# A hybrid attention and mixture-of-experts block: a block's rows dealt over sixteen runs, and the late experts' weight loads put in another order

## The chip, the cores and the metric

One core of one Trainium2 chip runs the whole block. The metric is the device time of one execution in microseconds (us). Before the change it is 1148.38 us, the median of 3 runs (1148.19 to 1149.16). One further execution was profiled; every duration below comes from it.

## The reference, cut to what matters

The block first mixes tokens (a gated linear attention branch and an indexer-selected attention branch, joined by gates and an output projection), and then adds a mixture of experts. Only the second part is touched:

```python
def hier_moe(h, w_rg, b_rg, w_re, b_re, w_gate, w_up, w_down):   # h: 1024 tokens of 1024
    ...
    g_sel = jnp.argmax(g_logits, axis=-1)                        # one of 4 groups
    ...
    top_v, top_i = lax.top_k(e_in_group, EXPERT_TOPK)            # two of its 8 experts
    ...
    for e in range(N_EXPERTS):                                   # 32
        hid = jax.nn.silu(xf @ w_gate[e]) * (xf @ w_up[e])       # w_gate, w_up: 1024 x 128
        y = y + combine[:, e:e + 1] * (hid @ w_down[e]).astype(f32)   # w_down: 128 x 1024
    return y.astype(h.dtype).reshape(b, t, d)
```

Each token picks 2 experts, so 32 experts share 2,048 rows, 64 on average. Worked out from the reference on its own inputs, an expert gets between 44 and 93 rows; the last one to be computed gets 63, the one before it 90, the first one 48. All in fp32.

## The kernel before

**The block of an expert.** A block is a table of R = 96 row numbers for each of the 32 experts, one number to a partition. `place` fills it: a token that is the r-th of its expert is compared with the constant row `self.slot` (part of `onehot`, made in `_constants`, L85), and a product on TensorE puts the token's number into that partition whose `slot` equals r. Before the change `slot` is 0, 1, 2, ... 95, so an expert with 64 tokens fills partitions 0 to 63, and partitions 64 to 95 hold an out-of-range number. An expert with over 96 tokens would leave its rest to a loop at the end of `run`, which works from another table and is not entered with these inputs.

**Work of one expert** (`Moe.run`, the loop over j = 0 to 31, in the order `self.order`). An indirect DMA issued from GpSimd (`gather_x`, L1275) fetches the tokens' rows of 4 KB from `h2d` into 96 partitions; a row with an out-of-range number is not moved. TensorE transposes them (`xpose`, L1283). `split` (L1259 on ScalarE, L1260 on VectorE) turns the raw gate and up weights into a high and a low part in two buffers. `gate_up` (L1267) is 24 matmuls of 256 columns; then come the activation, a transpose (`hid_T`, L1303) and `down` (L1311), 4 matmul instructions on the raw down weights. A second indirect DMA (`scatter`, L1319) adds the rows, 4 KB each, to `out` in memory, again leaving out those out of range. The order of one step j is: `gate_up(j+1)`, `hid_T(j)`, `xpose(j+2)`, `gather_x(j+5)`, `down(j)`, `scatter(j)`, `split(j+2)`, `load(j+9)`.

**The weights.** An expert has three loads of 512 KB (`load`): gate (L1023), up (L1026), down (L1029), all issued on SP's queue. There are NR = 9 buffers, so the load of expert j+9 needs the buffer of expert j: its gate and up halves are free once `split(j)` has read them, its down part only after `down(j)`. Gate and up also wait until a gather issued shortly before has landed (`late`). SP issues strictly in its order, and the tile framework gives its DMAs eight semaphores in turn, so an issue also waits until the load eight places ahead in SP's order has landed in full. The order on SP is made by the framework's scheduler from the program's order and from what each load waits for; a `SCHED` dependency between two instructions only fixes which stands first.

```python
        first = q = nc.sync.dma_start(raw[0][:, 0:1024], wg...)         # gate
        q = nc.sync.dma_start(raw[0][:, 1024:2048], wu...)              # up
        self.down = nc.sync.dma_start(raw[1], wd)                       # down
```

Of the kernel before, what the change touches and what calls it, by code (L numbers as in the profile page):

```python
# [21 lines left out]
SCHED = mybir.DependencyInfo(mybir.DependencyClass.NoSync, mybir.DependencyReason.SCHED_ONLY)  # L22
# [5 lines left out]
NT = T // P  # L28
# [5 lines left out]
R = 96  # L34
OOB = 1 << 20
NE = 32
# [7 lines left out]
def _bucket(rel):  # L44
    n = np.abs(rel)
    nf = np.maximum(n, 1).astype(np.float32)
    large = 8 + (np.log(nf / np.float32(8)) / np.float32(math.log(16.0)) * np.float32(8)).astype(np.int32)
    large = np.minimum(large, 15)
    return np.where(rel > 0, 16, 0) + np.where(n < 8, n, large)
# [12 lines left out]
def _constants():  # L62
    c = np.zeros((P, C_W), np.float32)
    p = np.arange(P)

    def put(name, v):
        o, w = _OFF[name]
        c[:, o:o + w] = v

    put("ident", np.eye(P))  # L70
    same = (p[:, None] // 64) == (p[None, :] // 64)
    put("suf", (p[:, None] > p[None, :]) & same)
    put("lt", p[:, None] < p[None, :])
    put("ones", 1.0)
    put("cmask", np.where((p[:, None] < 64) & (p[None, :] >= 64), NEG, 0.0))
    put("ind2", (p[:, None] // 64) == np.arange(2)[None, :])
    put("iota_e", np.arange(NE)[None, :])
    put("tok", p[:, None] + P * np.arange(NT)[None, :])
    put("tie8", 8 - np.arange(8)[None, :])
    put("tie4", 4 - np.arange(4)[None, :])  # L80
    put("thr", (np.arange(NB) + 1)[None, :] * R)
    put("pid", p[:, None])
    oh = np.zeros((P, 512 + R + NT), np.float32)
    oh[:, 384:512] = np.eye(P)[::-1]
    oh[:, -R - NT:-NT] = np.arange(R)[None, :]  # L85
    oh[:, -NT:] = p[:, None] + P * np.arange(NT)[None, :] - T
    rel = np.arange(383) - 255
    oh[_bucket(rel), np.arange(383)] = 1.0
    oh[15, :384] -= 1.0
    oh[15, 383] = 0.0  # L90
    return c, oh
# [893 lines left out]
class Moe:  # L985
# [27 lines left out]
        assert self.ko <= 20.75 * 256  # L1013
        return a

    def load(self, j, wg=None, wu=None, wd=None, late=None, after=None):
        nc = self.nc
        if wg is None:
            e = self.order[j]
            wg, wu, wd = self.w_gate[e], self.w_up[e], self.w_down[e]  # L1020
        raw = self.raws[j % len(self.raws)]

        first = q = nc.sync.dma_start(raw[0][:, 0:1024], wg.rearrange("(p k) c -> p (k c)", p=P))  # L1023
        if late:
            self.tc.add_manual_dep(q.ins, late.ins.name, SYNC, reason="the tokens' rows come first")
        q = nc.sync.dma_start(raw[0][:, 1024:2048], wu.rearrange("(p k) c -> p (k c)", p=P))  # L1026
        if late:
            self.tc.add_manual_dep(q.ins, late.ins.name, SYNC, reason="the tokens' rows come first")
        self.down = nc.sync.dma_start(raw[1], wd)  # L1029
        for q in (first, q, self.down) if after else ():  # L1030
            self.tc.add_manual_dep(q.ins, after.ins.name, SCHED, reason="order of loads")
        return raw
# [213 lines left out]
    def run(self, vp, ch, dump, stop):  # L1246
# [8 lines left out]
        def split(j, raw, late=False):  # L1255
            hi, lo = (t.rearrange("p (k n c) -> p n k c", k=KT, n=2) for t in WG[j % 2])
            for n in range(2):
                r = raw[0][:, 1024 * n:1024 * n + 1024].rearrange("p (k c) -> p k c", k=KT)
                nc.scalar.activation(hi[:, n], r, AF.Copy)  # L1259
                q = nc.vector.tensor_sub(lo[:, n], r, hi[:, n].bitcast(F32))  # L1260
                if late:
                    tc.add_manual_dep(q.ins, self.routed.ins.name, SCHED, reason="routing first")
# [9 lines left out]
        gathered = {}  # L1272

        def gather_x(j, idx):
            gathered[j] = nc.gpsimd.indirect_dma_start(out=XG[j % 4][:R], out_offset=None, in_=self.h2d,  # L1275
                                         in_offset=bass.IndirectOffsetOnAxis(ap=idx, axis=0),
                                         bounds_check=T - 1, oob_is_err=False)
            return gathered[j]

        def xpose(j):  # L1280
            pt = self.bankA(f"pxg{j}").rearrange("p a (b t) -> p (a b) t", b=4)
            xg = XG[j % 4]
            qs = [nc.tensor.transpose(pt[:, k, :R], xg[:R, k * P:(k + 1) * P], ident[:R, :R]) for k in range(KT)]  # L1283
            xh, xl = (t.rearrange("p (k t) -> p k t", k=KT) for t in XT[j % 2])
            nc.scalar.activation(xh, pt[:, :, :R], AF.Copy)  # L1285
            self.xl = nc.vector.tensor_sub(xl, pt[:, :, :R], xh.bitcast(F32))  # L1286
            return qs[0]

        def gate_up(j):
            w = [t.rearrange("p (k c) -> p k c", k=KT) for t in WG[j % 2]]  # L1290
            x = [t.rearrange("p (k t) -> p k t", k=KT) for t in XT[j % 2]]
            pg = self.bankB(f"pgu{j}")
            last = mm3(pg[:R, :256], [([t[:, k, :] for t in x], [t[:, k, :] for t in w]) for k in range(KT)])
            th, hd = HD[j % 2][:, 0:P], HD[j % 2][:, P:2 * P]
            nc.scalar.activation(th[:R], pg[:R, :P], AF.Tanh, scale=0.5)  # L1295
            nc.vector.scalar_tensor_tensor(hd[:R], th[:R], 1.0, pg[:R, :P], op0=ALU.add, op1=ALU.mult)
            nc.vector.tensor_mul(hd[:R], hd[:R], pg[:R, P:256])
            return last

        def hid_T(j):  # L1300
            hd, hT = HD[j % 2][:, P:2 * P], HD[j % 2][:, 2 * P:3 * P]
            ph = self.bankC(f"phd{j}")
            nc.tensor.transpose(ph[:, :R], hd[:R], ident[:R, :R])  # L1303
            nc.scalar.activation(hT[:, :R], ph[:, :R], AF.Copy)  # L1304

        def down(j, raw, wgt):
            hT = HD[j % 2][:, 2 * P:3 * P]
            for half in range(2):
                py = self.bankB(f"py{j}{half}")
                s = slice(512 * half, 512 * half + 512)  # L1310
                nc.tensor.matmul(py[:R], hT[:, :R], raw[1][:, s], start=True, stop=True)  # L1311
                av = AC[j % 4][:R, s]
                if half:
                    nc.scalar.activation(av, py[:R], AF.Copy, scale=wgt)  # L1314
                else:
                    nc.vector.tensor_scalar(av, py[:R], wgt, None, op0=ALU.mult)  # L1316

        def scatter(j, idx):
            return nc.gpsimd.indirect_dma_start(out=self.out, out_offset=bass.IndirectOffsetOnAxis(ap=idx, axis=0),  # L1319
                                                in_=AC[j % 4][:R], in_offset=None, bounds_check=T - 1, oob_is_err=False,  # L1320
                                                compute_op=ALU.add)

        def apart(a, g):

            for q in range(4):
                if q != g:
                    for b in done.get(q, []):
                        tc.declare_no_dep(a.ins, b.ins, reason="tokens of another group")
            done.setdefault(g, []).append(a)
# [8 lines left out]
        NR = len(self.raws)  # L1338
# [10 lines left out]
        first = gate_up(0)  # L1349
# [3 lines left out]
        for j in range(NE):  # L1353
            if j + 1 < NE:
                gate_up(j + 1)
            hid_T(j)
            if j + 2 < NE:
                xpose(j + 2)
                if j + 5 < NE:
                    gather_x(j + 5, idx(j + 5))  # L1360
            down(j, raw(j), wgt(j))
            apart(scatter(j, idx(j)), self.order[j] // 8)
            if j + 2 < NE:
                split(j + 2, raw(j + 2))
            if j + NR < NE:
                self.load(j + NR, late=gathered.get(min(j + 3, NE - 1)) if j > 1 else None)
            if j == 4:
                self.blocks(dump)
            if j == 9:
                tc.add_manual_dep(nc.gpsimd.drain().ins, gathered[j + 5].ins.name, SCHED, reason="after the gather")  # L1370
            if j == NE - 3:
                ntot = nc.values_load(self.lrow[0:1, 3:4], min_val=0, max_val=24)  # L1372
# [48 lines left out]
```

## Time and profile before

| what | us or share |
|---|---|
| median of 3 runs | 1148.38 (1148.19 to 1149.16) |
| the profiled execution, its own time | 1146.56 |
| its span, first to last instruction | 1144.8 |
| TensorE (PE) busy | 1077.3, 94% |
| VectorE (DVE) busy | 880.6, 77% |
| ScalarE (ACT) busy | 502.7, 44% |
| GpSimd (POOL) busy | 299.4, 26% |
| mean granted TensorE clock | 0.977 of full speed |
| time on the DMA engines of SP's loads and stores (q1) | 29.5% of 16 engines |
| the same of GpSimd's DMAs (q0) | 6.7% of 16 engines |

The shares are averages over a long program; the experts are its last fifth, from about 930 us on. A share of DMA is the time that packets took, over 16 DMA engines. The profile gives no engine's own share, only their mean, and a load has landed only when the slowest of its 16 engines is done.

### The profile page before, as it was taken

Reading aid. Unit: us, or ns where it says so; the run is one execution under the profiler, and the core shown is the slowest. Engines: PE = TensorE matmul, PEld = TensorE weight load, DVE = VectorE, ACT = ScalarE, POOL = GpSimd, SP = SyncE. Lnnn points to the kernel's source line nnn. Section 1 sums busy time; section 2 is a strip of 40 time slices with the busy share of each in tenths; the row PEclk is TensorE's granted clock in tenths of the full one; section 3 lists DMA queues with packets and bytes.
Section 4 is the critical chain, followed back from the end, with each engine's and each line's share of the span. In section 5 each row is a group of like instructions: output and inputs, shape, how many; then the busy total and the mean of one; then the engine's idle time right before and its main releaser. Section 6 shows DMA issues by size and latency. Waiting matters only on the chain. (4 is left out here: it accounts for less than half of the span.)

```text
span 1144.8 us, 18016 instructions
## 1 busy us (share of the span) xinstructions
PE 1077.3 (94%) x6652; PEld 895.1 (78%) x6652; DVE 880.6 (77%) x1742; ACT 502.7 (44%) x1110; POOL 299.4 (26%) x240
## 2 busy tenths in 40 slices
PE   6999999899999999999989999999999859999785
PEld 5998898788788888989767878887777747777563
DVE  5679999999999999994487786373566758878563
ACT  6566627032221124653588775121222226666352
POOL 0110025231122120312043210052011255487332
PEclk9999999999999999999999999999999959999898
DMA  7111120134223221200001015486442578999894
GB/s 260 38 38 38 38 75 4 48 103 164 74 91 111 92 79 51 74 1 1 19 20 38 19 39 186 147 282 211 147 147 83 186 251 228 300 314 265 251 289 81
DMA packets 73133, 139.81 MB, mean 122 GB/s; under 512 B 12315, under 2 KB 47444, under 8 KB 73044
## 3 DMA queue, kind: packets, MB, share of 16 engines
q1 hardware_dynamic: 62772, 112.40, 29.5%
q0 software_dynamic: 7968, 17.86, 6.7%
q10 hardware_dynamic: 2304, 8.39, 1.9%
q8 instruction: 53, 0.87, 0.3%
q14 instruction: 36, 0.29, 0.1%
HBM read 115.24 MB, written 31.76 MB: 128 GB/s over the span
## 5 line engine op out<-in xcount | busy, mean ns | idle before, releaser
L747 DVE MAX8 G<-G 128x8 f32<-128x384 f32 (+5 forms) x192 | 171.1, 893 | 5.0
L748 DVE MATCH_REPLACE8 G<-G 128x384 f32<-128x384 f32 (+5 forms) x192 | 168.1, 876 | 0.0
L236 PE MATMUL pg<-Qa,Q 128*128 128x512 f32 x512 | 159.8, 392 | 0.0
L228 POOL TENSOR_TENSOR Q<-G,Q 128x2048 fp32r<-128x2048 f32 x13 | 60.1, 4626 | 210.5 <-ACT Q L227 210.5
L236 PEld LDWEIGHTS pg<-Qa,Q 128*128 128x128 f32 x512 | 96.0, 188 | 20.9 <-issue 0.9
L236 PE MATMUL pg<-Qb,Q 128*128 128x512 f32 x256 | 99.6, 389 | 0.0
L227 ACT ACTIVATE Q<-G 128x2048 fp32r<-128x2048 f32 x19 | 36.3, 1911 | 78.4 <-PE pg L236 76.8
L236 PE MATMUL pv<-Q,Qa 128*128 128x256 f32 x352 | 65.0, 285 | 0.0
L1319 POOL DMA_INDIRECT out_dram<-G x24 | 47.7, 1986 | 64.8 <-ACT G L1314 21.2
L630 POOL TENSOR_TENSOR sm<-Tb,G 128x256 f32<-128x256 f32 x48 | 35.3, 738 | 98.4 <-DVE G L648 64.3
L1267 PE MATMUL pgu<-Qb,xt1h 128*96 128x256 f32 x256 | 52.9, 305 | 4.3 <-ACT xt1h L1285 3.7
L236 PEld LDWEIGHTS pv<-Q,Qa 128*128 128x128 f32 x352 | 55.2, 191 | 1.5 <-issue 1.0
L1260 DVE TENSOR_TENSOR Qb<-G,Qb 128x1024 fp32r<-128x1024 f32 x38 | 45.7, 1216 | 13.7 <-ACT Qb L1259 13.2
L236 PEld LDWEIGHTS pg<-Qb,Q 128*128 128x128 f32 x256 | 48.1, 188 | 10.4 <-issue 0.5
L1267 PE MATMUL pgu<-Qb,xt0h 128*96 128x256 f32 x256 | 53.7, 311 | 0.9 <-issue 0.9
L1275 POOL DMA_INDIRECT xg<-h2d,G x32 | 47.0, 1467 | 26.4 <-PE pxg L1283 8.1
L653 ACT ACTIVATE sm<-sm,G 128x128 f32<-128x128 f32 (+7 forms) x64 | 49.3, 772 | 7.0 <-DVE G L648 6.5
L1267 PEld LDWEIGHTS pgu<-Qb,xt1h 128*96 128x96 f32 x256 | 39.2, 175 | 14.6 <-ACT xt1h L1285 13.6
L236 PE MATMUL pv<-Q,Qb 128*128 128x256 f32 x176 | 49.7, 283 | 0.0
L814 POOL TENSOR_TENSOR G<-G 128x512 f32<-128x512 f32 x16 | 24.3, 1526 | 92.4 <-DVE G L813 92.4
L662 PE MATMUL pPT<-G,sm 128*128 128x128 f32 x288 | 44.6, 279 | 2.7 <-ACT sm L653 1.1
L577 ACT ACTIVATE G<-pg 128x1024 f32<-128x1024 f32 x16 | 16.3, 1019 | 69.2 <-issue 41.4
(369 smaller groups left out, 2982.5 us busy)
## 6 DMA issues: line engine op xcount, KB each, us to landing
G<-in_w_in_dram SPq DMA_DIRECT2D x19, 1024.0 KB
G<-in_w_down_dram SPq DMA_DIRECT2D x19, 512.0 KB
G<-in_w_gate_dram SPq DMA_DIRECT2D x19, 512.0 KB
G<-in_w_up_dram SPq DMA_DIRECT2D x19, 512.0 KB
gd<-G SPq DMA_DIRECT2D x16, 512.0 KB
G<-gd SPq DMA_DIRECT2D x16, 512.0 KB
raw<-in_w_gate_dram SPq DMA_DIRECT2D x9, 512.0 KB
raw<-in_w_up_dram SPq DMA_DIRECT2D x9, 512.0 KB
```

The source lines that it names most:

```text
L227: nc.scalar.activation(hi, r3, AF.Copy)
L228: (eng or nc.vector).tensor_sub(lo, r3, f(hi))
L236: q = nc.tensor.matmul(o, a, b, start=(i == 0), stop=(i == len(seq) - 1))
L630: nc.gpsimd.tensor_tensor(band, Tb[:, h, :], sc[i][:, n1:], op=ALU.add)
L653: nc.scalar.activation(sm[:, :W], sm[:, :W], AF.Exp, scale=-1.0, bias=nm[:, 1:2], accum_out=rs8s[i][:, h:h + 1])
L662: nc.tensor.transpose(pt[:, b, :], sm[:, (b0 + b) * P:(b0 + b + 1) * P], ident)
L747: nc.vector.max(out=m8, in_=sc[i])
L748: nc.vector.match_replace(out=sc[i], in_to_replace=m8, in_values=sc[i], imm_value=SENT)
L1260: q = nc.vector.tensor_sub(lo[:, n], r, hi[:, n].bitcast(F32))
L1267: q = nc.tensor.matmul(o, a, b, start=(i == 0), stop=(i == len(seq) - 1))
L1275: gathered[j] = nc.gpsimd.indirect_dma_start(out=XG[j % 4][:R], out_offset=None, in_=self.h2d, in_offset=bass.IndirectOffsetOnAxis(ap=idx, ...
L1319: return nc.gpsimd.indirect_dma_start(out=self.out, out_offset=bass.IndirectOffsetOnAxis(ap=idx, axis=0), in_=AC[j % 4][:R], in_offset=Non ...
```

## The change

Two edits. First, `slot` becomes a deal: partition s takes the token of rank (s mod 6) * 16 + s div 6. The 96 partitions are seen as sixteen runs of six, and ranks 0 to 15 go to the first partition of each run, 16 to 31 to the second, and so on. An expert with 64 tokens now has four rows in each run of six, at partitions 0 to 3, 6 to 9, 12 to 15 and so on. Second, from expert 18 on (counted from 0) each gate load is made to stand behind the down load of the expert ahead, and each down load behind the up load of its own expert.

```diff
     oh[:, 384:512] = np.eye(P)[::-1]
-    oh[:, -R - NT:-NT] = np.arange(R)[None, :]
+
+    s = np.arange(R)
+    oh[:, -R - NT:-NT] = (s % (R // 16) * 16 + s // (R // 16))[None, :]
     oh[:, -NT:] = p[:, None] + P * np.arange(NT)[None, :] - T
...
-    def load(self, j, wg=None, wu=None, wd=None, late=None, after=None):
+    def load(self, j, wg=None, wu=None, wd=None, late=None, after=None, turns=False):
...
+        if turns:
+
+            self.tc.add_manual_dep(first.ins, self.down.ins.name, SCHED, reason="the expert ahead comes first")
         self.down = nc.sync.dma_start(raw[1], wd)
+        if turns:
+            self.tc.add_manual_dep(self.down.ins, q.ins.name, SCHED, reason="the expert's parts in order")
...
-                self.load(j + NR, late=gathered.get(min(j + 3, NE - 1)) if j > 1 else None)
+                self.load(j + NR, late=gathered.get(min(j + 3, NE - 1)) if j > 1 else None, turns=j + NR >= 18)
```

On PE, VectorE, ScalarE and GpSimd the two programs have the same instructions in the same order. On SP the loads are the same, in another order from expert 18 on. The first place is SP's queue in the middle of the loop. `in_w_gate`, `in_w_up` and `in_w_down` are the sources; `rawx`, `raw5`, `raw6` and `raw7` are the buffers of the experts that leave a remainder of 2, 5, 6 and 7 by 9, and `G` holds the other five. Before, from the gate load of expert 18 on:

```order
L1023 DMA G_69<-in_w_gate_dram 128x1024
L1026 DMA G_69<-in_w_up_dram 128x1024
L1029 DMA raw7_7767<-in_w_down_dram 128x1024
L1023 DMA G_69<-in_w_gate_dram 128x1024
L1026 DMA G_69<-in_w_up_dram 128x1024
L1029 DMA G_69<-in_w_down_dram 128x1024
L1023 DMA rawx_6642<-in_w_gate_dram 128x1024
L1026 DMA rawx_6642<-in_w_up_dram 128x1024
L1029 DMA G_69<-in_w_down_dram 128x1024
```

These are gate and up of expert 18, down of 16 (`raw7`), gate and up of 19, down of 17, gate and up of 20 (`rawx`), down of 18, and so on: gate and up go two experts ahead of down. After the change, the same place, beginning with down of 15 (`raw6`):

```order
L1034 DMA raw6_7554<-in_w_down_dram 128x1024
L1028 DMA G_69<-in_w_up_dram 128x1024
L1034 DMA raw7_7767<-in_w_down_dram 128x1024
L1028 DMA G_69<-in_w_up_dram 128x1024
L1034 DMA G_69<-in_w_down_dram 128x1024
L1025 DMA G_69<-in_w_gate_dram 128x1024
L1028 DMA rawx_6642<-in_w_up_dram 128x1024
L1034 DMA G_69<-in_w_down_dram 128x1024
L1025 DMA G_69<-in_w_gate_dram 128x1024
L1028 DMA G_69<-in_w_up_dram 128x1024
L1034 DMA G_69<-in_w_down_dram 128x1024
L1025 DMA rawx_6642<-in_w_gate_dram 128x1024
```

The order is now up 18, down 16, up 19, down 17, gate 18, up 20, down 18, gate 19, up 21, down 19, gate 20 (`rawx`). Up and down stand where they stood; a gate load has moved two experts back, to the place that the gate of the expert after next had. The second place is the end of SP's queue. Before, from gate and up of expert 30 on:

```order
L1023 DMA G_69<-in_w_gate_dram 128x1024
L1026 DMA G_69<-in_w_up_dram 128x1024
L1029 DMA G_69<-in_w_down_dram 128x1024
L1023 DMA G_69<-in_w_gate_dram 128x1024
L1026 DMA G_69<-in_w_up_dram 128x1024
L1029 DMA rawx_6642<-in_w_down_dram 128x1024
L1029 DMA G_69<-in_w_down_dram 128x1024 x2
```

After, from the gate load of expert 29 (`rawx`) on:

```order
L1025 DMA rawx_6642<-in_w_gate_dram 128x1024
L1028 DMA G_69<-in_w_up_dram 128x1024
L1034 DMA rawx_6642<-in_w_down_dram 128x1024
L1025 DMA G_69<-in_w_gate_dram 128x1024
L1034 DMA G_69<-in_w_down_dram 128x1024
L1025 DMA G_69<-in_w_gate_dram 128x1024
L1034 DMA G_69<-in_w_down_dram 128x1024
```

Before, up of 31 was the last load ahead of three downs. Now the gates of 30 and 31 stand between these downs, and gate 31 is the last load but one.

## Rows read from the trace of the kernel before

**Rows 1.** The page's 40 slices of the span: TensorE, clock, DMA engines
```profile
PE   6999999899999999999989999999999859999785
PEclk9999999999999999999999999999999959999898
DMA  7111120134223221200001015486442578999894
```

**Rows 2.** Stretches: length, busy time by engine (count), clock, DMA share, GB/s
```profile
960.00:1055.00 95.00, 93.86 (x647) 73.71 (x646) 76.79 (x105) 62.69 (x106) 61.78 (x35) 1.00 0.95 285
1055.00:1075.00 20.00, 17.85 (x123) 13.95 (x122) 12.66 (x18) 9.36 (x15) 9.25 (x6) 1.00 0.88 253
1075.00:1095.00 20.00, 14.72 (x76) 10.73 (x75) 9.99 (x14) 8.72 (x14) 5.44 (x4) 0.74 0.89 261
1095.00:1115.00 20.00, 16.61 (x100) 12.25 (x97) 12.53 (x18) 11.17 (x20) 6.54 (x4) 0.91 0.93 303
```

**Rows 3.** Timeline of PE: where gate and up of experts 5, 21, 31 begin
```profile
965.17 0.56 PE L1267 MATMUL pgu<-Qb,xt1h 128*96 128x256 f32 x2
...
1052.87 0.56 PE L1267 MATMUL pgu<-Qb,xt1h 128*96 128x256 f32 x2
...
1124.30 0.80 PE L1267 MATMUL pgu<-Qb,xt1h 128*96 128x256 f32 x2
```

**Rows 4.** Waits of ScalarE from 1055 to 1115: total, times, longest
```profile
ACT Qb L1259 <- DMA G<-in_w_gate_dram: 7.9, 3, 3.8
ACT Qb L1259 <- DMA raw<-in_w_gate_dram: 4.9, 2, 3.8
ACT Qb L1259 <- DMA raw<-in_w_up_dram: 4.6, 2, 2.7
ACT Qb L1259 <- DMA G<-in_w_up_dram: 3.0, 2, 2.1
```

**Rows 5.** Waits of SP's queue from 1040 to 1110, its first three
```profile
SPq L1023 <- DMA raw<-in_w_up_dram: 9.6, 3, 3.4
SPq L1023 <- DMA G<-in_w_up_dram: 8.9, 4, 3.4
SPq L1029 <- DMA raw<-in_w_gate_dram: 8.8, 3, 3.0
```

**Rows 6.** Timeline of SP: gates of experts 14, 25, 26, 27, 30; up of 31
```profile
973.02 0.34 SPq L1023 DMA_DIRECT2D raw<-in_w_gate_dram  x1
...
1046.39 0.33 SPq L1023 DMA_DIRECT2D raw<-in_w_gate_dram  x1
...
1056.67 0.33 SPq L1023 DMA_DIRECT2D G<-in_w_gate_dram  x1
...
1066.91 0.33 SPq L1023 DMA_DIRECT2D G<-in_w_gate_dram  x1
...
1093.75 0.33 SPq L1023 DMA_DIRECT2D G<-in_w_gate_dram  x1
...
1102.33 0.33 SPq L1026 DMA_DIRECT2D G<-in_w_up_dram  x1
```

**Rows 7.** DMA queues from 973 to 1118: packets, MB, share of 16 engines
```profile
q1 hardware_dynamic: 7873, 28.67, 57.2%
q0 software_dynamic: 5104, 12.08, 35.3%
```

**Rows 8.** The same from 1003 to 1010, when only weights flow
```profile
q1 hardware_dynamic: 738, 2.69, 96.9%
```

**Rows 9.** A stretch in which the last scatter alone runs, columns as above
```profile
1137.20:1138.20 1.00, 0.00 (x0) 0.00 (x0) 0.00 (x0) 0.00 (x0) 0.00 (x0) 0.50 0.60 115
```

**Rows 10.** The longest wait of PE from 915 to 965
```profile
PE pxg L1283 <- DMA xg<-h2d,G: 5.4, 1, 5.4
```

**Rows 11.** Timeline of ScalarE: the split of expert 31's weights
```profile
1118.07 1.99 ACT L1259 ACTIVATE Qb<-G 128x1024 fp32r<-128x1024 f32 x2
```

**Rows 12.** Chain that ended last: split of expert 30, matmuls of expert 29
```profile
1111.80 1.07 ACT Qb L1259
...
1114.03 0.96 DVE xt1l L1286
...
1115.03 2.83 PE pgu L1267 x22
```

## Prediction
> **What bounds the kernel now.** I read the page's slices first, then stretches of the experts' part, then who waits for whom, then the DMA queues.
>
> The slices [rows 1] show TensorE near full until the last six or seven, where it falls to 5 to 8 tenths, the clock dips, and the DMA engines are at their busiest. The stretches [rows 2] sharpen this: from 960 to 1055 TensorE is busy 93.86 of 95 us; in the three stretches of 20 us behind it 17.85, 14.72 and 16.61, and the granted clock falls to 0.74 and 0.91, that is, part of the time at 1.2 instead of 2.4 GHz, behind TensorE's idle time. So two stages: first TensorE is the bound, then something else.
>
> What it loses is read from three starts [rows 3]. Experts 5 to 21 begin from 965.17 to 1052.87, 16 steps of 5.48 us. Ten more steps from 1052.87 would let expert 31 begin at 1107.7; it begins at 1124.30. The late stage costs **16.6 us**, the clock's part included. What TensorE lacks are weights: ScalarE's split waits 7.9 + 4.9 + 4.6 + 3.0 = 20.4 us for gate and up loads between 1055 and 1115 [rows 4].
>
> Why are loads late? SP issues a load only when one issued earlier has landed [rows 5], and does so every 3.42 us (six loads between 1046.39 and 1066.91 [rows 6]). But an engine has 8 packets of 4 KB in a load. When only weights flow, 2.69 MB, 657 packets, take 96.9% of 16 engines for 7 us [rows 8]: 0.165 us a packet, 1.3 us a load. At the same time the engines' mean share is 0.88 to 0.95 [rows 2], at 253 to 303 GB/s. Loads that wait while engines have time left mean that a few engines are late and each load waits for them.
>
> The gathers and scatters can do this. If the 96 partitions are served in order, six to an engine, ranks 0 to 41, which every expert has (44 at least), fill the first seven engines, while the last five get little. A full engine then has 6 rows where the mean is 4. Check: from 973 to 1118 the queues moved 28.67 MB of weights and 12.08 MB of rows [rows 7], per engine 437 packets and 184 rows. A row took 35.3% x 145 x 16 / 2949 = 0.278 us. A full engine: 437 x 0.165 + 276 x 0.278 = 72 + 77 = 149 us, against the 145 that passed. I take this as the bound: seven or eight engines, full throughout. With the weight packets' price in this mixture, 57.2% x 145 x 16 / 7000 = 0.190 us, it would be 160, 10% too long; 0.165 is nearer.
>
> **The change, part by part.**
>
> *The deal.* It moves no byte, instruction or wait; each expert's rows spread over the sixteen runs, at most one row apart. By the experts' counts the fullest engine falls from 192 of the 2,048 rows to 143, the mean is 128. Fullest engine from 973 on: 72 + 184 x 143/128 x 0.278 = 72 + 57 = 129 us, scaled by what the check missed (145/149), **126 us: the last weights land at about 1099** instead of 1118. Bounds: evenly spread, 120 us, 1093; with 0.190 a packet, 83 + 57 = 140 us, 1113.
>
> *When they are needed.* At TensorE's pace expert 31 begins at 1107.7. Its split began 6.2 us ahead of its matmuls (1118.07 [rows 11], 1124.30 [rows 3]), so its gate is wanted at **1101.5**. I allow nothing beyond that: the chain [rows 12] runs from the split of expert 30 over VectorE's `xt1l` to the matmuls of expert 29, because ScalarE and VectorE work in order, and a late gate holds up the expert ahead of it too.
>
> *The order of loads.* What SP's queue holds is not quite what the words say: gate j stands behind down j-1, but up j and down j have stayed, so a gate comes two experts, six loads, later than before, and up waits for it idle. No wait is added: the down that a gate now follows is due to its buffer long before. But in a queue that is behind, six loads are time: 126 us over 56 loads is 2.25 us each, 13.5 us in the middle. There gate 28 has nine loads behind it, lands near 1099 - 20 = 1079, and is needed at 1101.5 - 3 x 5.48 = 1085; gate 25, with eighteen behind it, at 1059 for 1069. At the end gate 31 has one load behind it, where up 31 had three: it lands at about 1097, 4 us ahead of need, where the old order would have had 9. With the bound of 1113 it lands at 1111, 10 us late; with 1093, in time. I take **2 us** of new stalls, nearer the second, since the check favours 0.165.
>
> *The ends.* The first gather holds TensorE for 5.4 us [rows 10]; expert 0's 48 rows put 3 on an engine instead of 6, among other packets. At 0.165 to 0.278 a row that is 0.5 to 0.8 us, up to twice that if weight packets alternate with them, nothing if they are not the last: 0 to 1.5, I take 0.5. The last scatter has 63 rows, 4 instead of 6 in the fullest run. With it alone, 115 GB/s are 28 rows in a microsecond on 0.60 of 16 engines [rows 9], 0.34 us a row: 0.7 us saved at the very end (0.5 to 1). That share fits 63 rows dealt six to an engine (10.5 of 16, 0.66) better than an even spread.
>
> *The sum:* 1146.56 (the profiled execution) - 16.6 - 0.7 - 0.5 + 2 = **1130.8**. That execution is 1.8 us under the median, within what single runs differ by; I put the forecast at **1131.5**.
>
> *A rule against it.* The row: the mean share of 0.60 with one scatter of 63 rows running [rows 9], and the 145 us that six rows to an engine nearly explain [rows 7]. The Trainium skill's page "DMA: Bandwidth & Descriptors", section "The descriptor swizzle", says that in a transfer of 128 partitions engines 0 to 7 serve partitions 0 to 63, in groups of four, and 8 to 15 the rest. If that held for these 96, runs of six would be no engine's share, and the deal would spread the rows only in part; by it the sum would be that of the third rival.
>
> **The rivals.**
>
> 1. *Weights stay the bound.* With 0.190 us a packet, gate 31 lands at 1111, 10 us after 1101.5: 1146.56 - 16.6 - 1.2 + 10 = 1139, with the median's offset **1140**. For it: the DMA share is at 0.93 from 1095 to 1115 already, little room if all that time is real work. Against: the check fits the lower price.
>
> 2. *Slower: the deal relieves nothing, and late gates cost.* If the full engines stay full, gate 25, issued at 1046.39, goes where gate 27 went, 1066.91 [rows 6], 20 us later, and at the end the gate of 30, once issued at 1093.75, stands behind up 31, issued at 1102.33. That one was there for its split by 1119 or so [rows 11], 7 us after the split of expert 30 began [rows 12]. A microsecond may hide: 1148.4 + 6 = **1154**. It decides if the fullest engine gains less than about 4 us in 145. For it: no view shows single engines. Against: the share under 1 while every load is waited for, and the check.
>
> 3. *Rows dealt by groups of four.* Partitions 0 to 63 on eight engines: before, 8 of 64 rows on each of these, 72 + 368 x 0.278 = 174 us, 20% over what passed, so the rows speak against it. After, four of every six partitions are filled, 5.3 rows an engine: 72 + 245 x 0.278 = 140 us, the last weights at 1113 and **1140**. This is what the skill's swizzle would make of this kernel.
>
> 4. *The two edits cancel:* relief of 4 to 8 us, spent by later gates: **1148**.
>
> **How the numbers follow.** About 0.2%, 2.3 us, is what a measurement of this kernel can tell from no change. The forecast, 1126 to 1135, gets 0.67; rival 1 0.16, rival 3 0.04, rival 2 0.08, rival 4 0.05. Faster: 0.67 + 0.16 + 0.04 = 0.87; same 0.05; slower 0.08. The low end is the sum without new stalls, with the larger gains at both ends (16.6 + 1.0 + 1.5, so 1127.5) and the median no higher than a profiled execution, rounded down to 1126; the high end takes in rivals 1 and 3 and stops short of rivals 2 and 4: 1142.
>
> **What would show it.** Right: expert 31 begins near 1107 to 1109; from 1055 to 1110 TensorE is as busy as before 1055 and the clock stays at 1.00; ScalarE's waits for gate and up loads fall from 20.4 us to a few; SP issues a load every 2.2 to 2.5 us and GB/s rise over 300; the last weights land at 1095 to 1105. The waits that remain should name gates, not ups, since gates are what the new order makes late. Wrong: SP still spaced by 3.4 us (the deal relieves nothing, rival 2), or a high DMA share with splits waiting for gates (rival 1), or a new wait of TensorE on gathers.

## The result, and the profile after

The changed kernel takes 1131.97 us (median of 4 runs, 1130.81 to 1134.32) against 1148.29 us for the kernel before in the same comparison (4 runs, 1146.62 to 1149.16): a ratio of 0.9862, 95% interval 0.9842 to 0.9883. Its profiled execution took 1132.71 us. The forecast of 1131.5 is 0.5 us off, and that is partly luck: two of its terms were wrong in opposite directions, as the experiments show.

The slices of the page after, against [rows 1]: in slice 38 TensorE rises from 7 to 9 tenths, the clock from 8 to 9 and the DMA engines from 8 to 9. The dip of slice 33 is in both; a slice is some 28 us long, so that one lies ahead of expert 5.

```profile
span 1130.9 us, 18002 instructions
...
PE   6999999899999999999999999999999959999985
...
PEclk9999999999999999999999999999999979999998
DMA  8111120125222321200000112565543297999993
```

The stretches, with the columns of [rows 2]: length, busy time by engine with counts, clock, DMA share, GB/s.

```profile
960.00:1055.00 95.00, 93.88 (x642) 73.28 (x640) 77.01 (x106) 62.81 (x107) 62.75 (x36) 1.00 1.03 311
1055.00:1075.00 20.00, 17.72 (x123) 13.57 (x121) 14.07 (x19) 12.20 (x20) 10.18 (x7) 1.00 1.05 322
1075.00:1095.00 20.00, 19.00 (x133) 15.27 (x133) 14.52 (x21) 11.42 (x21) 8.55 (x5) 1.00 1.03 330
1095.00:1115.00 20.00, 17.79 (x105) 13.54 (x103) 11.67 (x17) 9.06 (x17) 7.09 (x4) 0.91 0.40 89
```

The DMA engines move 311 to 330 GB/s in the first three stretches, where it was 253 to 285, and the bytes are through earlier: from 1095 on the DMA share is 0.40. TensorE is nearly full again from 1075 to 1095, but not from 1055 to 1075 nor behind 1095. Where expert 5 and expert 31 begin their matmuls, against the first and last of [rows 3]:

```profile
962.01 0.56 PE L1274 MATMUL pgu<-Qb,xt1h 128*96 128x256 f32 x2
...
1111.26 0.80 PE L1274 MATMUL pgu<-Qb,xt1h 128*96 128x256 f32 x2
```

That is 149.25 us for these 26 steps, after 159.13 before: 9.9 us of the span's 13.9 us. Another 3.2 us were saved ahead of expert 5, and 0.9 us behind the start of expert 31 (19.6 us to the end of the span, after 20.5). Expert 31 began at 1111.26, later than the 1107 to 1109 that the prediction gave as a sign. What ScalarE still waits for, from 1055 to 1115, against [rows 4] (engine and line, what it waited for, total, times, longest):

```profile
ACT Qb L1266 <- DMA G<-in_w_gate_dram: 5.4, 4, 2.3
ACT Qb L1266 <- SPq L1383: 2.1, 1, 2.1
ACT Qb L1266 <- DMA raw<-in_w_gate_dram: 0.4, 1, 0.4
```

20.4 us of waits for gate and up loads have become 5.8 us for gates, and none names an up load. The 2.1 us that the view puts down to SP's branch stand ahead of the split of expert 29 and are a gate's too: that gate was issued at 1073.46 and landed 18.7 us later, at 1092.2, as the split began. So the waits for gates come to 7.9 us.

```profile
1073.46 0.33 SPq L1025 DMA_DIRECT2D rawx<-in_w_gate_dram  x1
...
DMA to landing us min/median/max: 18.7/18.7/18.7
```

The timeline of ScalarE:

```profile
1083.82 1.06 ACT L1266 ACTIVATE Qb<-G 128x1024 fp32r<-128x1024 f32 x1 [0.83 <-DMA G<-in_w_gate_dram]
...
1092.28 2.01 ACT L1266 ACTIVATE Qb<-rawx 128x1024 fp32r<-128x1024 f32 x2 [2.10 <-SPq L1383]
1097.22 1.06 ACT L1266 ACTIVATE Qb<-G 128x1024 fp32r<-128x1024 f32 x1 [2.06 <-DMA G<-in_w_gate_dram]
...
1105.03 1.99 ACT L1266 ACTIVATE Qb<-G 128x1024 fp32r<-128x1024 f32 x2
```

These are the splits of experts 28, 29, 30 and 31. Those of 28 to 30 begin after an idle time; that of 31 does not.

### The profile page after: what moved, and what is told of

It reads as the page before. It is cut to its first block, busy times and chain, and to the rows that moved or that the text cites. A ratio compares the mean times of both kernels' runs of the same rounds, so it can differ in the third digit from the quotient of the medians.

```text
span 1130.9 us, 18002 instructions
## 1 busy us (share of the span) xinstructions
PE 1071.0 (95%) x6652; PEld 891.3 (79%) x6652; DVE 879.9 (78%) x1742; ACT 502.0 (44%) x1110; POOL 301.2 (27%) x240
## 4 chain that ended last, share of the span: by engine, by line
PE 66%; DVE 16%; DMA 10%; issue 4%; ACT 4%; SPq 0%; POOL 0%; POOLq 0%; DVEq 0%; ACTq 0%
PE pg L238 15%; PE py L238 8%; PE pw L238 5%; PE pgu L1274 5%; DVE G L750 4%; DVE G L749 3%; PE pav L677 3%; PE pqkv L238 3%; DMA G<-in_w_up_dram 3%; PE pPT L664 3%; PE pidx L238 3%; PE pv_None L238 2%; DMA raw<-in_w_gate_dram 2%; DVE G L419 2%; PE pk L238 2%
## 5 line engine op out<-in xcount | busy, mean ns | idle before, releaser
L1282 POOL DMA_INDIRECT xg<-h2d,G x32 | 50.9, 1590 | 24.9 <-DVE xt1l L1293 12.7
L1274 PE MATMUL pgu<-Qb,xt1h 128*96 128x256 f32 x256 | 50.4, 294 | 5.1 <-ACT xt1h L1292 5.1
```

What stands on the lines that cost most here:

```text
L1274: q = nc.tensor.matmul(o, a, b, start=(i == 0), stop=(i == len(seq) - 1))
```

## The experiments

Each table entry "5 to 31" is the time from the first matmul of expert 5 to that of expert 31 in the profiled execution, read from two rows like those above. It leaves out the start of the expert stage, which differs by up to 2.3 us between two executions of one kernel (below).

| kernel | rows | order of loads | median us | ratio to before, 95% interval | 5 to 31, us |
|---|---|---|---|---|---|
| before | in order | old | 1148.29 | 1 | 159.1 |
| the change | dealt | new | 1131.97 | 0.9862 (0.9842 to 0.9883) | 149.3 |
| the change, again | dealt | new | 1133.37 | 0.9892 (0.9876 to 0.9909) | 147.7 |
| deal only | dealt | old | 1126.15 | 0.9830 (0.9814 to 0.9845) | 141.9 |
| deal only, again | dealt | old | 1126.84 | 0.9824 (0.9807 to 0.9840) | 141.9 |
| order only | in order | new | 1151.29 | 1.0047 (1.0032 to 1.0063) | 165.0 |
| mirrored | in order, from the far end | old | 1141.37 | 0.9957 (0.9940 to 0.9974) | 155.6 |
| rotated | in order, from run 4 on | old | 1143.67 | 0.9971 (0.9952 to 0.9989) | 157.2 |
| dealt over 12 runs | dealt in part | old | 1139.88 | 0.9935 (0.9910 to 0.9960) | 151.5 |
| strict order | dealt | gate, up, down | 1131.28 | 0.9852 (0.9821 to 0.9882) | 144.7 |
| back and forth | dealt evenly | new | 1130.49 | 0.9854 (0.9830 to 0.9879) | 145.4 |
| back and forth, no wait for gathers | dealt evenly | old | 1125.29 | 0.9825 (0.9800 to 0.9851) | 141.9 |

The ratios of one group of runs share their runs of before: the deal alone, the order alone, the mirrored block and the repeat of the change; then strict, back and forth, 12 runs and rotated; then the deal again and the last row. The medians of before in these three groups are 1146.15, 1147.89 and 1146.80 us. Each profile is of one execution: that of the 12 runs is the fastest of its four, 2.9 us under their median, the others lie within 1.8 us of theirs.

### The deal alone, the order alone, and both again

```diff
 deal only
-... if j > 1 else None, turns=j + NR >= 18)
+... if j > 1 else None)
 order only
-    oh[:, -R - NT:-NT] = (s % (R // 16) * 16 + s // (R // 16))[None, :]
+    oh[:, -R - NT:-NT] = s[None, :]
```

> The deal of the rows alone, loads in the order of before. Theory (the deal relieves the full DMA engines, and the moved gate loads then cost): with both edits expert 31 began its matmuls 7.1 us behind the pace of experts 5 to 21 and the splits waited 5.8 us for gates; without the moved gates most of that goes, so 1126 to 1128 us, 4 to 6 us faster than both edits together. Rival (what is left is DMA time alone, the order costs nothing): 1131 to 1133, as with both. Second rival (part of the gain comes from the order): slower than 1134.

> The order of loads alone, rows not dealt. Theory (late gates cost in a queue that is behind): 1152 to 1158 us, slower than before by 4 to 10; splits wait for gates, expert 31 begins 4 to 10 us later than 1124.3. Rival (the order is neutral): 1147 to 1149. Rival (the order helps): under 1146.

> Both edits, unchanged, on the same chip as the runs beside it: 1131 to 1133 us by every theory.

Deal alone: 1126.15 us, inside the theory's range, and 7 us faster than both edits on the same chip, a little more than the 4 to 6 expected. Both edits again took 1133.37 us, 0.4 above what was expected. The two rows of expert 5 and 31:

```profile
962.24 0.56 PE L1274 MATMUL pgu<-Qb,xt1h 128*96 128x256 f32 x2
...
1104.13 0.80 PE L1274 MATMUL pgu<-Qb,xt1h 128*96 128x256 f32 x2
```

1104.13 - 962.24 = 141.89 us, 5.46 us a step; before, TensorE kept 5.48 from expert 5 to 21. The stretches of this kernel show it full to the end:

```profile
1055.00:1075.00 20.00, 19.75 (x141) 15.83 (x140) 16.42 (x22) 13.29 (x23) 12.55 (x8) 1.00 1.05 326
1075.00:1095.00 20.00, 19.75 (x134) 15.12 (x133) 15.84 (x23) 13.56 (x24) 9.03 (x6) 1.00 1.03 325
```

The view of ScalarE's waits from 1055 to 1115 names no weight load at all in this kernel. So the deal alone removes the whole late stall, 159.1 - 141.9 = **17.2 us**, and the order gives 6 to 7 us of that back (149.3 and 147.7 against 141.9).

Order alone: 1151.29 us, slower than before by 0.3 to 0.6%, and a little under the 1152 to 1158 that I had written. ScalarE from 1040 to 1125:

```profile
ACT Qb L1266 <- DMA G<-in_w_gate_dram: 14.3, 4, 7.1
ACT Qb L1266 <- DMA raw<-in_w_gate_dram: 5.8, 2, 4.2
```

Only gates are waited for, 20.1 us. The stall begins at expert 21 now, and the timelines show how it comes: ScalarE, held at the split of a later expert, has not yet made `xt1h`, the rows of this one. First ScalarE, then TensorE:

```profile
1057.45 1.06 ACT L1266 ACTIVATE Qb<-G 128x1024 fp32r<-128x1024 f32 x1 [7.12 <-DMA G<-in_w_gate_dram]
1058.41 0.79 ACT L1292 ACTIVATE xt1h<-pxg 128x768 fp32r<-128x768 f32 x1
```

```profile
1059.26 0.74 PE L1274 MATMUL pgu<-Qb,xt1h 128*96 128x256 f32 x2 [6.92 <-ACT xt1h L1292]
...
1129.14 0.80 PE L1274 MATMUL pgu<-Qb,xt1h 128*96 128x256 f32 x2
```

The order costs 165.0 - 159.1 = 5.9 us without the deal and 5.8 to 7.4 us with it. The rivals by which the order is neutral, or gives part of the gain, fall.

### Which rows share an engine

```diff
 mirrored (rank r at partition 95 - r)
+    oh[:, -R - NT:-NT] = (R - 1 - s)[None, :]
 rotated (rank r at partition r + 24, modulo 96)
+    oh[:, -R - NT:-NT] = ((s + 72) % R)[None, :]
```

Both stand in the deal's place, with the old order of loads.

> Loads in the order of before; rank r goes to partition 95 - r, so that partitions 32 to 95 are filled instead of 0 to 63. Theory of sixteen runs of six, each an engine's: the same loads on the engines in mirror order, fullest 192 rows, so 1147 to 1150 us and SP's issues still spaced by 3.4 us. Rival (groups of four, partitions 0 to 63 on eight engines and 64 to 95 on the other eight): the fullest engine falls from 256 to 173 rows, so 1126 to 1136.

> Loads in the order of before; rank r goes to partition r + 24, modulo 96, so that runs 4 to 11 are the full ones, 192 rows in the fullest, none dealt. The mirrored block (e3) was 5 us faster than before with the same 192. Theory (each run of six is one engine's, all engines alike): 1144 to 1149 us. Rival (the lowest engines, full in the block of before alone, are slower or have other work): 1138 to 1143, as mirrored. Rival (groups of four): 1125 to 1136.

Neither expectation was met to the letter. Mirrored took 1141.37 us, rotated 1143.67 (1142.03 to 1147.55), between the ranges. But the steps from 5 to 31 took 155.6 and 157.2 us, nearer to the 159.1 of before than to the 141.9 of the deal, and SP's issues are still far apart. In the mirrored kernel, with the same columns as [rows 6]:

```profile
1044.69 0.33 SPq L1025 DMA_DIRECT2D raw<-in_w_gate_dram  x1
...
1054.35 0.33 SPq L1025 DMA_DIRECT2D G<-in_w_gate_dram  x1
...
1063.94 0.33 SPq L1025 DMA_DIRECT2D G<-in_w_gate_dram  x1
```

Six loads in 19.25 us, 3.21 us a load, where before it was 3.42. Groups of four, as in the third rival, fall with this: by them the mirrored block would have had a fullest engine of 173 rows and the deal one of 202, so the mirror should have been the faster of the two, and it was 15 us slower. Runs of six explain the order of all these kernels.

No view shows a single engine, but the last scatter, 63 rows alone on the engines, shows how rows are served. First before, then with the rows dealt over twelve runs (next section), then with the deal alone, from its first packet to its last:

```profile
1136.10:1139.30 3.20, 0.00 (x0) 0.00 (x0) 0.00 (x0) 0.00 (x0) 0.00 (x0) 0.63 0.62 86
```

```profile
1126.80:1129.70 2.90, 0.00 (x0) 0.00 (x0) 0.00 (x0) 0.00 (x0) 0.00 (x0) 0.55 0.67 89
```

```profile
1115.95:1118.25 2.30, 0.00 (x0) 0.00 (x0) 0.00 (x0) 0.00 (x0) 0.00 (x0) 0.88 0.87 112
```

The share rises and the scatter gets shorter. In the trace's records of these packets, 11 are most often open at once before, 10 or 11 mirrored and rotated, 12 with twelve runs and 16 with the deal alone. Rows in order, six to an engine, need 11 engines for 63 rows; groups of four would put them on 8 before and on all 16 mirrored.

Runs of six do not explain why runs 0 to 7 in full cost some 2 to 3.5 us more than runs 8 to 15 or 4 to 11. The scatter of single profiles (two of the change differ by 1.6 us) may be part of it, but not all: by the medians both kernels are faster than before, with intervals that stay under 1. The rival by which the lowest engines are slower or have other work is not ruled out.

### The dose

```diff
 dealt over the first twelve runs
+    oh[:, -R - NT:-NT] = np.where(s < 72, s % 6 * 12 + s // 6, s)[None, :]
 every second round backwards, with the new order
+    oh[:, -R - NT:-NT] = (s % (R // 16) * 16 + np.where(s % (R // 16) % 2,
+                          15 - s // (R // 16), s // (R // 16)))[None, :]
```

> Loads in the order of before, rows dealt over the first twelve runs of six only; the fullest engine gets 175 rows (192 before, 143 with the full deal). Theory (the fullest engine sets the landing): its time from 973 on falls by 77 x 17/192 = 7 us, so the last loads land near 1111 and the splits still wait: 1130 to 1138 us, between 1126 and 1146 to 1148. Rival (any spread removes the stall): 1125 to 1128. Rival (the fullest engine does not matter): 1145 to 1149.

> Both edits, but every second round of the deal runs backwards over the sixteen runs, so the fullest engine gets 130 rows instead of 143 of 2,048 (mean 128). Theory (what is left with both edits is late gates, on the fullest engine's time): some 13 rows of each direction less, 3 to 5 us of its time, so gates land that much earlier: 1128 to 1131 us. Rival (the fullest engine no longer decides, SP's waits do): 1132 to 1134.

Counted from the experts' rows, the fullest run holds 192 of the 2,048 rows before, 175 with twelve runs, 143 with the deal, 130 back and forth. With the old order the late stall is 17.2, 9.6 and 0 us for the first three: it falls with the fullest run. (The 9.6 come from the fastest of four executions; by the medians, twelve runs gain 8.0 us where the deal gains 20.0.) The time with twelve runs, 1139.88 us, is 2 us above the range I gave; both rivals fall. Back and forth with the new order took 1130.49 us, inside the theory's range; the steps take 145.4 us, 2.3 to 3.8 us less than the change. That points to the fullest engine in what is left with the change too, but the intervals of the two ratios overlap, so the times alone do not show it.

### The order that the words describe

```diff
         q = nc.sync.dma_start(raw[0][:, 1024:2048], wu.rearrange("(p k) c -> p (k c)", p=P))
+        if turns:
+            self.tc.add_manual_dep(q.ins, first.ins.name, SCHED, reason="up behind gate")
```

> The deal, and the order that the words of the change describe: up also stands behind its own gate, so from expert 18 on SP's queue is gate, up, down, gate, up, down, one expert after the other. Theory (what counts is how many loads stand ahead of the later of gate and up): in the old order the up of expert 18 is the 54th load of the loop's list, here the 56th, with the change as built the gate is the 57th. So two of the three places are lost: 1129 to 1131.5 us, between the deal alone (1126.2) and both edits (1132 to 1133.4). Rival (only the gates' two experts matter, or the up loads that go ahead are the harm): 1125 to 1128. Rival (it is no better than the change): 1131.5 to 1135.

From expert 18 on SP's queue is then truly gate, up, down, and the next gate. It took 1131.28 us (1128.31 to 1133.7), by the median within the theory's range, but the runs spread from just below it into that of the second rival. The steps are clearer: 144.7 us, 2.8 us of stall where the change has 5.8 to 7.4 and the old order none. That is in line with the count of loads ahead of the later of gate and up, though one profile of each is thin evidence.

### The best version

```diff
 deal back and forth as above, the old order, and
-                self.load(j + NR, late=gathered.get(min(j + 3, NE - 1)) if j > 1 else None, ...)
+                self.load(j + NR)
```

> Best attempt: old order of loads, the deal with every second round backwards (fullest engine 130 rows instead of 143), and no wait of gate and up loads for the gathers. Theory (with the deal alone TensorE is the bound from expert 5 to 31, steps of 5.44 us, so a faster DMA side has nothing left to give): 1125 to 1128 us, the same as the deal alone. Rival (the DMA side still costs at the start or the end): 1121 to 1124. Rival (the wait for the gathers protected them; without it TensorE waits for rows): over 1129.

> The deal alone again, on the chip of the run beside it: 1125 to 1128 us by every theory; whether expert 5 begins nearer 962 or 965 shows how much of the start differs from run to run of one kernel.

1125.29 and 1126.84 us, ratios 0.9825 and 0.9824: the same. But the best attempt's runs fall into two groups, three from 1124.24 to 1125.29 and two at 1129.82 and 1130.11; the profile is of the fastest, and what the slower two lost stays open. The more even deal and the missing wait for the gathers together do bring the loads forward (gate 31 is issued at 1071.93, with the deal alone at 1077.71), but TensorE takes steps of 5.46 us throughout in both kernels and cannot use it; the rows of the best attempt:

```profile
961.02 0.55 PE L1274 MATMUL pgu<-Qb,xt1h 128*96 128x256 f32 x2
...
1102.91 0.80 PE L1274 MATMUL pgu<-Qb,xt1h 128*96 128x256 f32 x2
```

So nothing tried is clearly faster than the deal without the order, 1126.15 us, which is the change less its second edit.

## Why the prediction was right, and where not

**The bound: right.** A few DMA engines, full of token rows, held up the weight loads. The dealt kernels show it: the late stall follows the rows of the fullest run and goes entirely once these are spread, and the last scatter shows the runs of six. One line of the evidence was misread: the 5 tenths of slice 33 belong to the stage ahead of expert 5, not to the late one.

**The late stall, 16.6 us: right.** The deal alone takes 17.2 us out of the steps from 5 to 31.

**"New stalls 2 us": the term that failed, too small by a factor of three.** The order costs 5.8 to 7.4 us. The mechanism was the one forecast, gates and only gates; the landing times under it were not. Gate 25 was to land at 1059 for 1069. Issued at 1042.88, it took 22.4 us and landed at 1065.3, and at TensorE's pace from 962.01 it was wanted at 962.01 + 20 x 5.46 - 6.2 = 1065.0. (Expert 5 began 3.2 us sooner than before, so the need came sooner too.) So the margin was used up at gate 25 already. I looked for the trouble at gate 31 and put 4 us of margin there; its split waits for nothing. I had gate 28 landing at 1079 for 1085; its split began at 1083.82 and was wanted, by the same working, at 1081.4. Those of 29 and 30, wanted at 1086.8 and 1092.3, began at 1092.28 and 1097.22, 5 us late. The deal alone shows how little room there was without the order: up 31, forecast 9 us ahead of need, was issued at 1079.05 and landed at 1097.9, about 1 us ahead of the second half of its split:

```profile
1079.05 0.33 SPq L1028 DMA_DIRECT2D G<-in_w_up_dram  x1
...
DMA to landing us min/median/max: 18.8/18.8/18.8
...
1097.90 1.99 ACT L1266 ACTIVATE Qb<-G 128x1024 fp32r<-128x1024 f32 x2
```

The step behind it was to space 56 loads evenly over 126 us, 2.25 us each. From gate 25 to gate 27 they went more slowly, as SP's timeline of the kernel after shows:

```profile
1042.88 0.33 SPq L1025 DMA_DIRECT2D raw<-in_w_gate_dram  x1
...
1052.05 0.33 SPq L1025 DMA_DIRECT2D G<-in_w_gate_dram  x1
...
1059.65 0.33 SPq L1025 DMA_DIRECT2D G<-in_w_gate_dram  x1
```

16.77 us for six loads, 2.8 us each, where the sign was 2.2 to 2.5; the deal alone has much the same (1037.67 to 1046.42 to 1055.68 for its gates, 3.0 us). Part of the time may have been lost earlier, between 990 and 1015, where SP waits for gathers before it may ask for up loads and what stands behind them:

```profile
SPq L1028 <- DMA xg<-h2d,G: 24.4, 4, 12.9
```

In the longest of these waits the queue ran low; the DMA view from 998 to 1014 falls to 82 GB/s in one of its slices. The prediction did not count this wait. It does not matter for the deal alone, which waits as long (24.5 us from 990 to 1020) and still takes its steps of 5.46 us; it may have cost the change some of its margin, but with the new order it was not tried without it.

**The ends.** Behind expert 31 0.7 us were forecast, and 0.9 came: 20.5 us to the end of the span before, 19.6 in the change and in the deal alone, 20.4 with the order alone. From the first packet to the last, the last scatter took 3.1 us before and 2.3 with the deal, some 0.45 us for each of the two rows fewer, where 0.34 was put. At the start 0.5 us was forecast and 3.2 came in the profiled execution, the error that hid the other one: with what was measured the sum is 1146.56 - 17.2 - 0.9 - 3.2 + 7.4 = 1132.7, against 1130.8 forecast for such an execution. The first wait for a gathered row, 5.4 us in [rows 10], is 4.0 in the change:

```profile
PE pxg L1290 <- DMA xg<-h2d,G: 4.0, 1, 4.0
```

In the seven profiles with the rows dealt over all runs it is 4.0 to 5.7 us, 4.8 on the mean; in the four with rows in order 5.4 to 6.8, 5.9 on the mean. That is some 1.2 us, with overlap. The rest differs between executions of one kernel, and so is put down to chance here. The stretch from 935 to 960, first in the deal alone, then in its repeat:

```profile
935.00:960.00 25.00, 23.26 (x162) 19.09 (x161) 20.20 (x35) 13.69 (x22) 14.60 (x10) 0.96 0.77 207
```

```profile
935.00:960.00 25.00, 23.44 (x146) 19.27 (x146) 19.75 (x35) 13.80 (x22) 13.75 (x9) 0.88 0.71 199
```

TensorE is as busy in both, but the granted clock is 0.96 and 0.88, that is, more of the second stretch passed at 1.2 GHz, and the second one finished fewer instructions (146 for 162). Expert 5 begins at 962.24 and 963.50.

**The rivals.** The slower one, late gates with no relief, was forecast at 1154, 6 us over before, and is what the order alone does: 1151.29, 5 us over its own runs of before. Weights as the lasting bound (1140) did not come: by its 0.190 us a packet gate 31 was to land at 1111, and its split began at 1105.03 without a wait. The two edits do pull against each other, as the fourth has it, but with 17.2 us against 5.8 to 7.4 they do not cancel. The swizzle of the Trainium skill, "DMA: Bandwidth & Descriptors", "The descriptor swizzle", is given there for 128 partitions; these scatters of 96 do not follow it (11 packets open at once for 63 rows, not 8), and neither do the times of the mirrored kernel.

## What to carry to other kernels

When loads are waited for while the DMA engines' mean share leaves room, ask which engine carries most. Here an indirect transfer whose valid rows stood together put them on a few engines, and the weight loads came late with the fullest of these. Dealing the valid rows over the engines' runs adds no instruction and moved this kernel by 1.7 to 1.8%. And look at what a scheduler makes of an ordering edge: pinning a gate behind the down load ahead did not bring the expert's three loads together, it moved the gate two experts back, and in a queue with about 1 us of room that cost 5.8 to 7.4 us.

## What the runs showed of the hardware that I had not expected

The mean DMA share of 16 engines goes over 1: 1.05 from 1055 to 1075 in the change and in the deal alone. So packets on one engine overlap in this count, and a mean share of 0.9 was further from full than it looked. The times of packets in a mixture hold some of that overlap. Up 31, with three loads behind it in the deal alone, would by the price from the mixture (0.190 us) have landed at about 1105, by the price from weights alone (0.165 us) at about 1092, both estimates from the prediction's sums; it landed at 1097.9, so neither price holds as it is.

In these scatters of 96 partitions six neighbours go to one engine, and rows that are left out leave their engines idle: 63 rows in order keep some 11 packets open at once and take 3.1 us, the same rows dealt 16 and 2.3 us.

Which runs of six are full is not quite indifferent: 17.2 us of late stall with runs 0 to 7 full, 13.7 with 8 to 15, 15.3 with 4 to 11. No run here tells why.

A program's own start differs: the same kernel began expert 5 1.3 us apart in two executions (962.24 and 963.50), and the change 2.3 us apart (962.01 and 964.27), with the granted clock of that stretch.
